# A recurrent and attention decoder trunk on one core: three early weight transfers on ScalarE's queue, fewer warm-up products, and an explicit order for the recurrent section

## The chip, the core and the metric

The kernel runs on one core of a Trainium2 chip. The metric is the device time of one execution in microseconds. The kernel before takes 560.62 us, the median of three runs (560.37 to 561.4).

## What is computed

The reference is a trunk of two layers on x of 256 positions by 1024 channels in float32. Layer 0 has a recurrent mixer (RG-LRU), layer 1 an attention mixer; each is followed by an MLP with a squared ReLU. The change lies in layer 0's mixer, which is this:

```python
h = _rmsnorm(x, norm_mix[0])
proj = h @ w_in                                   # 1024 -> 2048
y = gelu(proj[..., :D_RNN])                       # gate branch
xb = causal_depthwise_conv(proj[..., D_RNN:], conv_w, conv_b)   # width 4
r = sigmoid(einsum(xr, w_a) + b_a)                # 4 blocks of 256, xr is xb by blocks
i = sigmoid(einsum(xr, w_x) + b_x)
log_a = -RG_C * r * softplus(-lam)
u = sqrt(-expm1(2 * log_a)) * (i * xb)
hs = associative_scan(a = exp(log_a), u)          # along the positions
x = x + (hs * y) @ w_out
```

After it come the MLP of layer 0, the attention layer, its MLP and a last RMSNorm, which the change does not touch.

## The kernel before, in words

Activations lie transposed: a tile of 128 channels by 256 positions is a chunk, and x is eight chunks, `xt[:, 0]` to `xt[:, 7]`. Weights stream from memory in pieces of 128 by 1024 float32 (512 KB), in the order in which they are used, into five buffers `raw0` to `raw4`. One piece holds the eight 128 by 128 blocks of one chunk of outputs.

Products are made in three passes of a rounded format, so that float32 accuracy is kept. Every operand is split: a high part is a copy in fp32r (`split`, L426 for a cast on ScalarE or VectorE), a low part is the difference of the raw value and the high one (L423, VectorE only). There are seven pairs of buffers for split weights, called `whl` in the profile. The products of one block are high by high, high by low and low by high: `mm3`, lines L413, L414 and L415, each with 256 columns. A projection of a chunk is 8 × 3 = 24 products. In the MLP two of the three passes go together (`mm2`, L419 and L420).

The input goes through the norm's gain alone first: `hh[:, k]` is the high part of g·x (ScalarE, L681) and `hl[:, k]` the low part (VectorE, L683); the factor 1/rms of each position is applied to the results, when the sums of squares (squares on ScalarE, L687) are known.

The recurrent section consists of steps that are put into a plan by `add`, with the engine, the step's keys for reading and writing, and a due time. Then `emit` gives each engine its instructions in the order of the plan. In the kernel before, the plan comes from a list scheduler fed with a row of random seeds (`SEED`). Later sections use an explicit list of step numbers (`ORDER`): the same `emit` runs the steps just in the order listed, and a prime behind a number takes the step's second engine. Each engine runs its own instructions strictly in order, and waits where an operand is not there.

The steps of the section, in their rough order:

- the first transfers (`FIRST`), below;
- c0 to c7, the eight chunks of the convolution branch (`conv`). c0, c1 and c2 are made together, interleaved by k (the chunk of x), in steps of three products, while the inputs come in. Their weights are split by quarters of a piece, two blocks each; quarter q of piece i has the high part hi*i.q* and the low part lo*i.q*;
- g0 to g3, the gates (`gate`): 32 plain float32 products (64 records at L790), tanh and exp on ScalarE, products on VectorE;
- y0 to y7, the gate branch (`branch`), the scan on VectorE (`scan`), gelu and the product with y (`product`);
- out0 to out7, the projection back, with the residual and the norm for the MLP;
- the first three chunks of the MLP's up projection and the splits of six more pieces (`lead_in`).

The first transfers are written in `FIRST` as tags. x0+ is chunks 0 and 1 of x (256 KB), x2+, x4+ and x6+ the other pairs. A tag of two digits is a weight quarter: 00 is quarter 0 of piece 0 (128 KB); a plus adds the quarter behind it, so 10+ is quarters 0 and 1 of piece 1 (256 KB). `piece` is a whole piece, `vec` and `cst` are small vectors and constants:

```python
FIRST = "x0+ 00 01 x2+ 10+ 20+ x4+ 02+ x6+ 12+ 22+ piece vec cst piece"
```

All of these are issued by SyncE (SP) in this order; only the first eight columns of `vec`, the norm's gain, are issued by ScalarE (L655), ahead of its first step, a table load. While nothing has landed, TensorE multiplies a tile of zeros (`warm`, L675), `WARM` = 26 times.

Of the kernel before, what the change touches and what calls it, by code (L numbers as in the profile page):

```python
# [14 lines left out]
AF = mybir.ActivationFunctionType  # L15
# [6 lines left out]
D = 1024  # L22
# [56 lines left out]
TRANSFER = {"raw": (2.0, 1.4, 0.6), "cast": (1.6, 2.2, 0.4), "add": (2.4, 3.0, 0.5), "move": (1.4, 0.21, 0.3)}  # L79
PLACED = "ks0 kw0 q0 q1 q2".split()  # L80
NI, NFINE = 3, 3
SQN = 2
# [228 lines left out]
def trunk_kernel(ctx: ExitStack, tc: tile.TileContext, x_in, vec_in, const_in, w2_in, wts, out):  # L311
    nc = tc.nc
    ctx.enter_context(tc.manual_schedule())
    pe, dve, act, pool = nc.tensor, nc.vector, nc.scalar, nc.gpsimd
# [22 lines left out]
    raw_t = [rpool.tile([P, WMAX], F32, name="raw%d" % i) for i in range(NRAW)]  # L337
# [96 lines left out]
    class Section:  # L434


        def __init__(self, carried=True):
            flush()
            self.carried = carried
# [5 lines left out]
        def transfer(self, kind, q, d, fn, t, r=(), w=()):  # L445

            pre, took, post = TRANSFER[kind]
            if not self.carried:
                self.add(q, 1.5, fn, r=r, w=list(w) + ["loads"], t=t, lag=2.0)
                return  # L450
            self.add(q, d, fn, r=r, w=list(w) + ["loads"] * (kind == "raw"), t=t, lag=pre)
# [69 lines left out]
        def proj(self, name, idx, b, t, step, xs=None, xk=None):  # L521
            wh, wl, wk = self.weight(name, idx, t)
            z = self.bank((name, idx), b, zcols)
            xs, xk = xs or [(hh[:, k], hl[:, k]) for k in range(KC)], xk or hkey
            for i in range(4):
                def run(e, i=i):
                    for k in (2 * i, 2 * i + 1):
                        w = slice(k * P, (k + 1) * P)
                        mm3(z(), wh[:, w], wl[:, w], xs[k][0], xs[k][1], k == 0, k == KC - 1)
                self.add("pe", 0.67 if self.carried else 0.68, run, r=wk + list(xk[2 * i:2 * i + 2]), w=[("ps", b)], t=t + i * step)  # L530
            return z, ("ps", b)

        def table(self, func, t):
# [2 lines left out]
        def stats(self, srcs, t):  # L536

            b6 = [("ps", 6)]
            st = self.bank(("stats", t), 6, lambda x: x)
            for j, (x, k) in enumerate(srcs):  # L540
                self.add("pe", 0.44, lambda e, j=j, x=x: square_sums(st(), x, j == 0, j == len(srcs) - 1), r=[k], w=b6, t=t)
            self.add("act", 0.2 if self.carried else 0.15, lambda e: e.activation(rcol, st()[:, :2], AF.Sqrt, bias=epst, scale=1.0 / D), r=b6 + ["tab"],
                     w=["rcol"], t=t)
            self.add("dve", 0.1 if self.carried else 0.08, lambda e: e.reciprocal(rcol, rcol), w=["rcol"], t=t)
# [46 lines left out]
    rcol = spool.tile([P, 2], F32, name="rcol")  # L591
# [43 lines left out]

    with ExitStack() as ph:
        rg = ph.enter_context(tc.tile_pool(name="rg", bufs=1))
        sec = Section(False)
# [6 lines left out]
        def first_load(q, o, i, key, d):  # L645
            add(q, d, lambda e: (nc.scalar if e is act else nc.sync).dma_start(o, i), w=key + ["loads"] * (q == "sp"), t=-29.0, lag=1.9)
# [8 lines left out]
        nc.scalar.dma_start(vec[:, :8], vec_in[:, :8])  # L655
# [123 lines left out]
        def gate(b, t):  # L779
            ms = (2 * b, 2 * b + 1)  # L780
            xk = [("xb", m) for m in ms]
            for mo, m in enumerate(ms):
                for which, d, nm in ((0, r_t, "r"), (1, i_t, "i")):
                    bk = nextbank()
                    z = sec.bank(("gate", m, which), bk, zcols)

                    def run(e, z=z, which=which, mo=mo):
                        for k in range(2):
                            o = ((which * 2 + mo) * 2 + k) * P
                            e.matmul(z(), gw[b][:, o:o + P], xb[2 * b + k], start=k == 0, stop=k == 1)  # L790
                    add("pe", 0.87, run, r=[("gw", b)] + xk, w=[("ps", bk)], t=t + PJ * (2 * mo + which))
# [775 lines left out]
```

## Time and profile before

| | |
|---|---|
| median of three runs | 560.62 us |
| the profiled execution | 560.43 us |
| its span, first to last instruction | 558.6 us |
| granted TensorE clock, mean | 0.997 |
| memory read | 101.36 MB, 183 GB/s over the span with what is written |

The span runs from the first to the last instruction on the core. Engines are PE (TensorE's products), PEld (its weight loads), DVE (VectorE), ACT (ScalarE), POOL (GpSimd) and SP (SyncE); SPq and ACTq are the queues on which SyncE and ScalarE issue DMAs. Times of instructions are in microseconds from the span's start. The records of products overlap, since they are pipelined: 0.28 us is the length of one of 256 columns, and dense products start much closer together than that. The recurrent section with the lead-in ends at about 95 us, where the first product of the MLP's own loop starts.

### The profile page before, as it was taken

Reading aid. Unit: us, or ns where it says so; the run is one execution under the profiler, and the core shown is the slowest. Engines: PE = TensorE matmul, PEld = TensorE weight load, DVE = VectorE, ACT = ScalarE, POOL = GpSimd, SP = SyncE. Lnnn points to the kernel's source line nnn. Section 1 sums busy time; section 2 is a strip of 40 time slices with the busy share of each in tenths; the row PEclk is TensorE's granted clock in tenths of the full one; section 3 lists DMA queues with packets and bytes.
Section 4 is the critical chain, followed back from the end, with each engine's and each line's share of the span. In section 5 each row is a group of like instructions: output and inputs, shape, how many; then the busy total and the mean of one; then the engine's idle time right before and its main releaser. Section 6 shows DMA issues by size and latency. Waiting matters only on the chain.

```text
span 558.6 us, 10523 instructions
## 1 busy us (share of the span) xinstructions
PE 547.1 (98%) x3862; PEld 515.5 (92%) x3862; DVE 454.8 (81%) x943; ACT 387.3 (69%) x793; POOL 51.0 (9%) x63
## 2 busy tenths in 40 slices
PE   8999999999999999999999998999999999999994
PEld 8999999999999999999999997999999999999994
DVE  6999999999996675676999999999999996565532
ACT  7699775877775553555799999977788776453420
POOL 1210000000000221221000101000000000132320
PEclk9999999999999999999999999999999999999998
DMA  8935466766566466556650767424777656466402
GB/s 290 407 131 189 151 223 194 261 200 211 193 196 221 151 207 216 180 192 225 242 182 16 211 160 238 102 42 153 241 241 231 216 196 227 153 190 220 156 1 75
DMA packets 32611, 105.19 MB, mean 188 GB/s; under 512 B 3984, under 2 KB 6944, under 8 KB 32560
## 3 DMA queue, kind: packets, MB, share of 16 engines
q1 hardware_dynamic: 30784, 99.70, 53.0%
q0 software_dynamic: 1200, 4.29, 3.3%
q8 instruction: 30, 0.49, 0.3%
q10 hardware_dynamic: 576, 0.53, 0.3%
q14 instruction: 21, 0.17, 0.1%
HBM read 101.36 MB, written 1.05 MB: 183 GB/s over the span
## 4 chain that ended last, share of the span: by engine, by line
PE 90%; ACT 5%; DVE 2%; DMA 1%; issue 1%; SPq 0%; DVEq 0%; ACTq 0%
PE bank L419 35%; PE bank L420 18%; PE bank L414 9%; PE bank L413 9%; PE bank L415 9%; PE bank L790 2%; ACT pt L1278 2%; PE bank L1308 1%; DMA xt<-in_dram 1%; ACT pth L1311 1%; PE bank L1335 1%; PE bank L1268 1%; PE bank L1140 1%; PE bank L1138 1%; PE bank L1139 1%
## 5 line engine op out<-in xcount | busy, mean ns | idle before, releaser
L369 DVE TENSOR_TENSOR whl<-raw,whl 128x1024 fp32r<-128x1024 f32 x117 | 146.5, 1272 | 5.5 <-ACT whl L360 3.1
L419 PE MATMUL bank<-hhl,whl 128*128 128x512 f32 x456 | 149.5, 382 | 0.0
L419 PE MATMUL bank<-uhl,whl 128*128 128x512 f32 x448 | 146.8, 382 | 0.0
L360 ACT CAST whl<-raw 128x1024 fp32r<-128x1024 f32 (+1 forms) x118 | 120.5, 1046 | 7.8 <-ACT whl L360 5.7
L420 PE MATMUL bank<-hhl,whl 128*128 128x256 f32 x456 | 124.3, 273 | 0.0
L420 PE MATMUL bank<-uhl,whl 128*128 128x256 f32 x448 | 122.1, 273 | 0.0
L419 PEld LDWEIGHTS bank<-hhl,whl 128*128 128x128 f32 x456 | 86.2, 189 | 11.9
L419 PEld LDWEIGHTS bank<-uhl,whl 128*128 128x128 f32 x448 | 84.7, 189 | 11.8
L413 PE MATMUL bank<-hhl,whl 128*128 128x256 f32 x312 | 87.9, 282 | 0.3 <-ACT hhl L681 0.3
L420 PEld LDWEIGHTS bank<-hhl,whl 128*128 128x128 f32 x456 | 87.6, 192 | 0.0
L414 PE MATMUL bank<-hhl,whl 128*128 128x256 f32 x312 | 86.1, 276 | 0.1
L420 PEld LDWEIGHTS bank<-uhl,whl 128*128 128x128 f32 x448 | 86.0, 192 | 0.0
L415 PE MATMUL bank<-hhl,whl 128*128 128x256 f32 x312 | 85.8, 275 | 0.0
L633 DVE TENSOR_TENSOR xt<-xt,bank 128x256 f32<-128x256 f32 x40 | 16.1, 417 | 72.2 <-ACT part L921 58.8
L423 DVE TENSOR_TENSOR whl<-raw,whl 128x1024 fp32r<-128x1024 f32 (+3 forms) x69 | 72.8, 1072 | 0.8 <-ACT whl L426 0.7
L426 ACT CAST whl<-raw 128x1024 fp32r<-128x1024 f32 (+2 forms) x61 | 57.0, 954 | 6.2 <-DMA raw<-in_dram 3.6
L414 PEld LDWEIGHTS bank<-hhl,whl 128*128 128x128 f32 x312 | 59.7, 191 | 0.9 <-DVE hhl L683 0.5
L413 PEld LDWEIGHTS bank<-hhl,whl 128*128 128x128 f32 x312 | 59.7, 191 | 0.7 <-ACT hhl L681 0.4
L415 PEld LDWEIGHTS bank<-hhl,whl 128*128 128x128 f32 x312 | 59.7, 191 | 0.0
L921 ACT COPY part<-bank 128x256 f32<-128x256 f32 x14 | 5.2, 372 | 61.8 <-PE bank L420 61.8
L893 ACT ACTIVATE u<-t 128x256 f32<-128x256 f32 x64 | 26.7, 418 | 12.3 <-DVE t L891 7.1
L886 ACT COPY b<-bank 128x256 f32<-128x256 f32 x57 | 20.9, 366 | 18.4 <-PE bank L420 18.3
(219 smaller groups left out, 1000.2 us busy)
## 6 DMA issues: line engine op xcount, KB each, us to landing
raw<-in_dram SPq DMA_DIRECT2D x171, 512.0 KB, 4.3
whl<-in_dram POOLq DMA_DIRECT2D x8, 512.0 KB, 5.4
gw<-in_dram SPq DMA_DIRECT2D x4, 512.0 KB, 8.9
raw<-in_dram SPq DMA_DIRECT2D x5, 256.0 KB, 5.4
xt<-in_dram SPq DMA_DIRECT2D x4, 256.0 KB, 4.9
zwol<-in_dram SPq DMA_DIRECT2D x2, 512.0 KB, 5.9
raw<-in_dram SPq DMA_DIRECT2D x2, 456.0 KB, 3.9
kh<-th SPq DMA_DIRECT2D x8, 64.0 KB, 5.1
```

The source lines that it names most:

```text
L360: (act.copy if eng is None else eng.tensor_copy)(hi_t[i % NSPL][:, :n], raw_t[i % NRAW][:, :n])
L369: (eng or dve).tensor_tensor(lo[:, :n], raw_t[i % NRAW][:, :n], hi[:, :n].bitcast(F32), op=OP.subtract)
L413: pe.matmul(ps, wh, xh, start=start, stop=False)
L414: pe.matmul(ps, wh, xl, start=False, stop=False)
L415: pe.matmul(ps, wl, xh, start=False, stop=stop)
L419: pe.matmul(z.rearrange("p (i b a) -> p i b a", i=2, a=2), wh, xd, start=start, stop=False)
L420: pe.matmul(pairs(z[:, :S]), wl, xd[:, 0], start=False, stop=stop)
L423: return lambda e: e.tensor_tensor(o, a, h.bitcast(F32), op=OP.subtract)
L426: return lambda e: (e.copy if e is act else e.tensor_copy)(o, a)
L633: dve.tensor_tensor(two(xt[:, m]), two(xt[:, m]), nat(z), op=OP.add)
L886: act.copy(two(b), nat(z[:, S:]))
L893: act.activation(u, t, AF.Square)
```

## The change

Four things are changed together.

1. Three of the first transfers, 00, 01 and 10+, are issued by ScalarE instead of SyncE, right behind its transfer of `vec`, and so ahead of its table load. The other transfers stay on SyncE in the order that they had.
2. `WARM` is 22 instead of 26.
3. The section's order comes from an explicit list of step numbers, `RG_STEPS`, and no longer from the scheduler with its seeds. The steps themselves are the same. A transfer is now two steps, the issue and the time on the DMA engines, and the second gives no instruction.
4. Some of the scheduler's costs are changed. With an explicit list they give no instruction and set no order.

The list of all 510 entries is cut here to its first two lines:

```diff
-SEED = (45, 94848, 51544, 88889, 49550, 67068, 32457, 33019)
+RG_STEPS = """
+1 5 4 8 2 111 112 6 9 0 11 13 15 17 53 19 32 54 21 29 33 59' 23 30 55' 60 25 35 113 56 38 27 114 36 61' 126 39 57' 127
+62 44 115 58 65' 116 63 41 128 66 129 71' 64 139 47 42 140 67' 72 141 73' 45 142 174 69' 117 48 43 118 50 68 119 74 40
...
+"""
-WARM = 26
+WARM = 22
...
         def first_w(i, q, n=2):
             w = wts[offs[i]:offs[i + 1]].rearrange("(h p n) -> h p n", h=2, p=P)[q // 2][:, q % 2 * 256:(q % 2 + n) * 256]
-            first_load("sp", raw_t[i][:, q * 256:(q + n) * 256], w, [("raw0", i, q + j) for j in range(n)], (0.47, 0.68)[n - 1])
-        sec.plan.busy["pool"] = 0.9
+            key = [("raw0", i, q + j) for j in range(n)]
+            if q + i < 2:
+                nc.scalar.dma_start(raw_t[i][:, q * 256:(q + n) * 256], w)
+                add("sp", 0.0, lambda e: None, w=key, t=-31, lag=3.2 + 0.4 * q + 1.2 * i)
+                return
+            first_load(raw_t[i][:, q * 256:(q + n) * 256], w, key, 0.34 * n)
+        sec.plan.busy.update(pool=0.9, sp=0.74, act=2.1, pe=5.2, dma=2.3)
...
-        sec.emit(SEED)
+        sec.emit(RG_STEPS)
```

With the steps' names in place of their numbers, the list begins like this on each engine:

- SyncE: x0+, x2+, 20+, x4+, 02+, x6+, 12+, 22+, piece, vec, cst, piece
- ScalarE: table load, hh1, hh0, hi0.1, hi1.0, hh2, hh3, hi1.1, hi2.0, hh5, hi0.2, hh4, hi0.3, hh6, hi1.2
- VectorE: hi0.0, lo0.0, hl1, hl0, lo0.1, lo1.0, hl2, hl3, lo1.1, lo2.0, hi2.1, lo0.2, lo2.1, hl4, lo0.3
- TensorE: c0 k0, c0 k1, c1 k0, c1 k1, c0 k2, c0 k3, c1 k2, c1 k3, c2 k0, c2 k1, c2 k2, c2 k3, c0 k4, c0 k5

Of the wide high parts of the pieces from c3 to the last of the lead-in, the list gives 26 to ScalarE and four to VectorE: those of y6 and of the up pieces 3, 5 and 7.

More of the change, by code (lines that the diff above doesn't have):

```diff
@@ L38 @@
 W1T, THS, THD, TPV, THT, NEARLY = 8.0, 10.5, 6.4, 44.0, 5.6, 6
-SEED = (45, 94848, 51544, 88889, 49550, 67068, 32457, 33019)
+RG_STEPS = """
+1 5 4 8 2 111 112 6 9 0 11 13 15 17 53 19 32 54 21 29 33 59' 23 30 55' 60 25 35 113 56 38 27 114 36 61' 126 39 57' 127
+62 44 115 58 65' 116 63 41 128 66 129 71' 64 139 47 42 140 67' 72 141 73' 45 142 174 69' 117 48 43 118 50 68 119 74 40
[6 rows of a table added]
+296 256 337' 241 288 229 258 272 346 289 338 268 243 259 266 245 273 347 260 297 267 270 269 262 274 303 246 271 390 329
[3 rows of a table added]
+445 352 369 490 383 394 368 498 387 432 384 417 385' 454 418 386 419 468 407 455 395 446 480 408 506 433 409 520 481 456
+411 492 420 434 524 457 447 421 469 410 422 396 448 470 399 449 482 412 508 493 458 500 459 423 528 483 397 460 435 501
+471 424 461 484 398 532 485 436 509 472 494 425 536 473 495 450 486 437 462 502 487 438 474 503 451 463 475 526 496 488
+464 510 476 477 504 522' 511 489 530' 497 514 512 523 515 505 516 540 534 517 538' 513 531 518 544 519 527 539 550 545
+552 542 543 546 535 554 556 547 548 549
+"""
 ORDER = """
@@ L76 @@
 RPEN = 0.51
-WARM = 26
+WARM = 22
 BY_DMA, DLEAD, NPEN = "o01 o03 o11 o13", 12.0, 0.3
-TRANSFER = {"raw": (2.0, 1.4, 0.6), "cast": (1.6, 2.2, 0.4), "add": (2.4, 3.0, 0.5), "move": (1.4, 0.21, 0.3)}
+TRANSFER = {"first": (1.5, 0.67, 0.7), "raw": (2.0, 1.3, 0.6), "cast": (1.6, 2.2, 0.4), "add": (2.4, 3.0, 0.5), "move": (1.4, 0.21, 0.3)}
 PLACED = "ks0 kw0 q0 q1 q2".split()
@@ L443, in __init__, with transfer @@
             self.zs = {}
-        def transfer(self, kind, q, d, fn, t, r=(), w=()):
+        def transfer(self, kind, q, d, fn, t, r=(), w=(), size=None):
             pre, took, post = TRANSFER[kind]
[L448 to L451, printed above, removed]
+            self.add(q, d, fn, r=r, w=list(w) + ["loads"] * (kind in ("raw", "first")), t=t, lag=pre)
             self.plan.carried[len(self.plan.tasks)] = len(self.plan.tasks) - 1
-            self.add("dma", took, lambda e: None, r=r, w=w, t=t, lag=post)
+            self.add("dma", took if size is None else size, lambda e: None, r=r, w=w, t=t, lag=post)
         def load(self, i, t):
@@ L529, in run @@
                         mm3(z(), wh[:, w], wl[:, w], xs[k][0], xs[k][1], k == 0, k == KC - 1)
-                self.add("pe", 0.67 if self.carried else 0.68, run, r=wk + list(xk[2 * i:2 * i + 2]), w=[("ps", b)], t=t + i * step)
+                self.add("pe", 0.67, run, r=wk + list(xk[2 * i:2 * i + 2]), w=[("ps", b)], t=t + i * step)
             return z, ("ps", b)
@@ L541, in stats @@
                 self.add("pe", 0.44, lambda e, j=j, x=x: square_sums(st(), x, j == 0, j == len(srcs) - 1), r=[k], w=b6, t=t)
-            self.add("act", 0.2 if self.carried else 0.15, lambda e: e.activation(rcol, st()[:, :2], AF.Sqrt, bias=epst, scale=1.0 / D), r=b6 + ["tab"],
+            self.add("act", 0.2, lambda e: e.activation(rcol, st()[:, :2], AF.Sqrt, bias=epst, scale=1.0 / D), r=b6 + ["tab"],
                      w=["rcol"], t=t)
-            self.add("dve", 0.1 if self.carried else 0.08, lambda e: e.reciprocal(rcol, rcol), w=["rcol"], t=t)
+            self.add("dve", 0.1, lambda e: e.reciprocal(rcol, rcol), w=["rcol"], t=t)
             self.add("pe", 0.22, lambda e: spread(st()), r=["rcol", "cst"], w=b6, t=t)
@@ L643, in trunk_kernel, with first_load @@
         table(AF.Sqrt, -30)
-        def first_load(q, o, i, key, d):
-            add(q, d, lambda e: (nc.scalar if e is act else nc.sync).dma_start(o, i), w=key + ["loads"] * (q == "sp"), t=-29.0, lag=1.9)
+        def first_load(o, i, key, took):
+            sec.transfer("first", "sp", 0.46, lambda e: e.dma_start(o, i), -29.0, w=key, size=took)
         def first_x(k, n=2):
-            first_load("sp", xt[:, k:k + n], x_in[k // 2], [("xt", k + i) for i in range(n)], (0.47, 0.68)[n - 1])
+            first_load(xt[:, k:k + n], x_in[k // 2], [("xt", k + i) for i in range(n)], 0.67 + 0.5 * (k == 2))
         def first_w(i, q, n=2):
             w = wts[offs[i]:offs[i + 1]].rearrange("(h p n) -> h p n", h=2, p=P)[q // 2][:, q % 2 * 256:(q % 2 + n) * 256]
-            first_load("sp", raw_t[i][:, q * 256:(q + n) * 256], w, [("raw0", i, q + j) for j in range(n)], (0.47, 0.68)[n - 1])
-        sec.plan.busy["pool"] = 0.9
+            key = [("raw0", i, q + j) for j in range(n)]
[5 more added lines that the diff above has]
+        sec.plan.busy.update(pool=0.9, sp=0.74, act=2.1, pe=5.2, dma=2.3)
         nc.scalar.dma_start(vec[:, :8], vec_in[:, :8])
-        add("sp", 0.0, lambda e: None, w=["vec0"], t=-31, lag=2.2)
+        add("sp", 0.0, lambda e: None, w=["vec0"], t=-31, lag=3.1)
         sec.seen.update(dma=NFINE, split=NFINE, lo=NFINE)
@@ L662, in trunk_kernel @@
             elif x == "cst":
-                first_load("sp", cst, const_in, ["cst"], 1.0)
+                first_load(cst, const_in, ["cst"], 0.78)
             elif x == "vec":
-                first_load("sp", vec[:, 8:], vec_in[:, 8:], ["vec"], 0.47)
+                first_load(vec[:, 8:], vec_in[:, 8:], ["vec"], 0.24)
             elif x[0] == "x":
@@ L790, in run @@
                             e.matmul(z(), gw[b][:, o:o + P], xb[2 * b + k], start=k == 0, stop=k == 1)
-                    add("pe", 0.87, run, r=[("gw", b)] + xk, w=[("ps", bk)], t=t + PJ * (2 * mo + which))
+                    add("pe", 0.865, run, r=[("gw", b)] + xk, w=[("ps", bk)], t=t + PJ * (2 * mo + which))
                     j = which * 8 + m
```

5 lines of the change are left out of this document (2 added, 3 removed), and 9 rows, old and new, of the table RG_STEPS.

## The prediction

> **What bounds the kernel now.** I read the page first: the span and the busy engines.
>
> ```profile
> span 558.6 us, 10523 instructions
> PE 547.1 (98%) x3862; PEld 515.5 (92%) x3862; DVE 454.8 (81%) x943; ACT 387.3 (69%) x793; POOL 51.0 (9%) x63
> ```
>
> TensorE (PE) is busy for 98% of the span. The profiled execution took 560.43 us, 1.8 us more than its span, and the median of the runs is 560.62 us, so a microsecond saved in the profile is a microsecond of the median. Next the windows view, by stage, for where PE is not busy. Its columns are the stretch, its length, busy time of PE, weight loads, VectorE (DVE), ScalarE (ACT) and GpSimd, the granted clock, the DMA engines' busy share and GB/s.
>
> ```profile
> core 0: us, PE busy (x) PEld busy (x) DVE busy (x) ACT busy (x) POOL busy (x), PEclk, DMA share, GB/s
> 0.00:1.50 1.50, 0.36 (x1) 0.37 (x2) 0.06 (x1) 0.33 (x1) 0.65 (x9) 1.00 0.00 0
> 1.50:3.50 2.00, 2.00 (x11) 2.00 (x11) 0.00 (x0) 1.16 (x2) 0.00 (x0) 1.00 0.77 205
> 3.50:5.00 1.50, 1.50 (x9) 1.50 (x9) 0.87 (x3) 1.12 (x3) 0.00 (x0) 1.00 0.72 175
> 5.00:12.00 7.00, 6.60 (x52) 6.04 (x51) 5.90 (x18) 5.54 (x17) 0.00 (x0) 1.00 1.00 365
> 12.00:30.00 18.00, 18.00 (x155) 17.70 (x154) 17.42 (x46) 13.48 (x25) 4.83 (x6) 1.00 1.00 390
> 30.00:56.00 26.00, 26.00 (x183) 24.55 (x182) 25.56 (x42) 25.59 (x47) 2.07 (x5) 1.00 0.44 153
> 56.00:95.00 39.00, 39.00 (x352) 39.00 (x351) 38.03 (x65) 28.32 (x45) 0.00 (x0) 1.00 0.53 178
> ```
>
> From 12 us to the end of the section at 95 us PE has no idle time, and DVE idles only 0.58 + 0.44 + 0.97 = 1.99 us. What a new order can win is therefore in the first 12 us, and what it can lose is anywhere after them. The DMA engines are full from 5 us on, but move only 205 and 175 GB/s between 1.5 and 5 us. The waits of the first 9 us (us in total, times, longest) say what PE lacks there:
>
> ```profile
> DVE whl L426 <- DMA raw<-in_dram: 3.2, 1, 3.2
> ACT hhl L681 <- DMA xt<-in_dram: 1.4, 1, 1.4
> DVE hhl L683 <- ACT hhl L681: 1.1, 1, 1.1
> PEld bank L414 <- DVE hhl L683: 0.5, 2, 0.3
> PEld bank L413 <- ACT hhl L681: 0.4, 1, 0.4
> ```
>
> PE waits for DVE and ACT, which make the high and low parts of x (hh, hl), and those wait for x in the DMA. The timeline of the same time shows the chain (start, length, engine, line, operation; SPq and ACTq are DMA issues):
>
> ```profile
> 0.73 0.41 ACTq L655 DMA_DIRECT2D vec<-in_dram  x1
> 0.74 0.39 SPq L646 DMA_DIRECT2D xt<-in_dram  x1
> 1.14 5.26 PE L675 MATMUL bank<-warm 128*128 128x256 f32 x26 [1.14 <-POOL xp L740]
> 1.18 1.28 ACT L534 ACT_TABLE_LOAD   x1 [1.18 <-PEq L1556]
> 1.18 0.89 SPq L646 DMA_DIRECT2D raw<-in_dram  x2
> 2.12 0.43 SPq L646 DMA_DIRECT2D xt<-in_dram  x1
> 2.59 0.91 SPq L646 DMA_DIRECT2D raw<-in_dram  x2
> 3.54 0.43 SPq L646 DMA_DIRECT2D xt<-in_dram  x1
> 3.88 0.91 ACT L681 ACTIVATE hhl<-xt,vec 128x256 fp32r<-128x256 f32 x2 [1.21 <-DMA vec<-in_dram]
> 4.09 0.29 DVE L426 CAST whl<-raw 128x256 fp32r<-128x256 f32 x1 [3.22 <-DMA raw<-in_dram]
> 4.42 0.48 DVE L683 SCALAR_TENSOR_TENSOR hhl<-xt,vec,hhl 128x256 fp32r<-128x256 f32 x1
> 5.05 0.48 DVE L683 SCALAR_TENSOR_TENSOR hhl<-xt,vec,hhl 128x256 fp32r<-128x256 f32 x1
> 5.44 0.76 DVE L423 TENSOR_TENSOR whl<-raw,whl 128x256 fp32r<-128x256 f32 x2
> 6.12 0.19 PEld L413 LDWEIGHTS bank<-hhl,whl 128*128 128x128 f32 x1
> 6.76 0.91 ACT L681 ACTIVATE hhl<-xt,vec 128x256 fp32r<-128x256 f32 x2 [1.35 <-DMA xt<-in_dram]
> ```
>
> In the order of the queue the transfers are x0+, 00, 01, x2+, 10+, 20+, x4+. The first product starts at 6.12; the second pair of x chunks (x2+, issued fourth) is there at 6.76. Counting the products that read the split weights:
>
> ```profile
> 6.12:8.43 2.31, 1.80 (x10) 1.00 0.98 337
> 8.43:12.83 4.40, 4.40 (x40) 1.00 1.04 395
> ```
>
> Dense, 40 products take 4.40 us, 0.11 each. In the 2.31 us before that only 10 were done, for 1.10 us of work: 1.2 us are lost. The first three pieces are 72 products, so they end at about 8.43 + 62 × 0.11 = 15.25 us.
>
> **The change, part by part.** *The three weight transfers.* 00, 01 and 10+ leave SP's queue for ACT's. On SP each issue takes 0.47 us (0.74, 1.18 and two, 2.12), so x2+ is issued at 1.18 instead of 2.12, and x4+ at about 2.1 instead of 3.54. On ACT three issues stand behind that of vec and take 3 × 0.43 = 1.3 us. Behind them is queued the table load, and behind that hh1 and hh0: the load ends near 0.73 + 4 × 0.45 + 1.28 + 0.1 = 3.9 us. ACT was idle for 1.21 us until 3.88, so this costs nothing; were x0+ there sooner than 3.6 us, it would cost the difference.
>
> *The first product.* The list has DVE make hi0.0 (high part of piece 0, quarter 0), lo0.0, hl1, hl0, in that order, and takes the casts of the other early quarters off it. If 00 lands at 4.1 to 4.6 us (4.09 before; it now shares the engines with x2+), the product follows after 0.33 + 0.38 + 0.40 + 0.40 + 0.1 = 1.6 us, at 5.7 to 6.2. I take 5.9: 0.2 us sooner.
>
> *The four warm-ups.* 26 of them take from 1.14 to 6.12, 0.19 each. The last four are worth between 4 × 0.11 = 0.44 and 0.76 us, so 22 end between 5.36 and 5.68, before the inputs are there. They take nothing off the sum by themselves; kept, they would hold the first product at 6.12.
>
> *What is late next: 10+.* The list puts two steps of piece 0 first (k0, k1: six products, 0.66 us), then k0 of piece 1, on PE; hi1.0 ahead of hh2 and hh3 on ACT; lo1.0 ahead of hl2 and hl3 on DVE. All three engines run in order, so x2+ is of no use until 10+ has landed. Call that time T. Then
>
> ```profile
> L426 ACT CAST whl<-raw 128x256 fp32r<-128x256 f32 x8 | 3.0, 395 | 0.1
> L423 DVE TENSOR_TENSOR whl<-raw,whl 128x256 fp32r<-128x256 f32 x12 | 4.5, 421 | 0.0
> ```
>
> the high part takes 0.40 and the low part 0.42 us, and the seventh product starts at T + 0.85. The remaining 66 products end at T + 0.85 + 66 × 0.11 = T + 8.1, if everything else is in time. Before it was 15.25. So the gain is 7.15 − T, and no more than the start allows: 15.25 − (5.9 + 72 × 0.11) = 1.4 us.
>
> For T, the landings (KB each, us from issue to landing; x0+, x2+, 10+, x4+):
>
> ```profile
> xt<-in_dram SPq DMA_DIRECT2D x1, 256.0 KB, 2.9
> xt<-in_dram SPq DMA_DIRECT2D x1, 256.0 KB, 4.6
> raw<-in_dram SPq DMA_DIRECT2D x1, 256.0 KB, 4.8
> xt<-in_dram SPq DMA_DIRECT2D x1, 256.0 KB, 5.2
> ```
>
> x0+ lands at 0.74 + 2.9 = 3.64. x2+ lands at 6.7 and x4+ at 8.74, with 10+ and 20+ between: three transfers of 256 KB in 2.0 us, 0.67 each, which is the full rate. x2+ itself comes 3.1 us behind x0+, though only 512 KB (1.35 us) lie between: there the engines had nothing to do, as the share of 0.72 says. 10+ is issued on ACT at about 2.05. It cannot be there before 2.05 + 2.9 = 4.95. Behind 00, 01 and x2+ it lands at 3.64 + 768 KB = 5.65; with 20+ ahead of it too at 6.3; with x4+ as well at 7.0. I take T = 5.9, between the second and the third and nearer to the second, since x2+ is issued 0.5 us before 20+ and two queues are served by turns. The gain is 7.15 − 5.9 = 1.25 us.
>
> *The others.* 20+, x4+, 02+ and what follows are issued 1.4 us sooner and land about 1 us sooner, because the rate is full from then on and only the empty time can be won. The list asks for 02+ fourth from there; if it is late by 0.5 us the gain is 0.75 us.
>
> *The order after 12 us.* It is the same set of steps. In the list ACT makes 26 of the 30 wide high parts and DVE four; before, ACT made all 30 up to 95 us. DVE has no such row, and its nearest one is the half-width cast:
>
> ```profile
> L426 ACT CAST whl<-raw 128x1024 fp32r<-128x1024 f32 x30 | 30.5, 1046 | 5.0 <-DMA raw<-in_dram 3.6 <-PE bank L414 1.4
> L426 DVE CAST xbh<-y 128x512 fp32r<-128x512 f32 x1 | 0.4, 429 | 0.0
> ```
>
> so four cost DVE at most 4 × 0.86 = 3.4 us, more than the 1.99 us that it idles after 12 us. Three of the four stand at the very end of the section, behind the last hl, where DVE no longer gates the last products; their cover is the start of the MLP, and if that is gone they cost up to 3 × 0.86 − 1.99 = 0.6 us. From below, a better order could win nothing, as PE has no wait there. I take 0, and for the range 0.4 us of loss. A gain in the section passes to the end: the stages behind it are chained by buffers and not by the clock.
>
> Sum: 560.43 − 1.25 = 559.2 for a profiled execution, 559.4 for the median.
>
> **The rivals.** All but one turn on T.
> (1) *Cover holds*, T below 5.7: the start limits, gain 1.4 to 1.7 us (with a first product at 5.7), 559.0. For it: x0+ lands 2.9 us after its issue, and 00 does too (1.18 to the cast at 4.09). Against it: 768 KB stand before 10+.
> (2) *The queues only take turns.* If SP's x2+, 20+ and x4+ are each served before ACT's next one, T = 7.0 and the gain is 0.15 us: 560.5. For it: the share of 1.00 from 5 us on, which no second queue raises. Against it: the 0.72 before. The Trainium skill, "DMA: Bandwidth & Descriptors", section "Issuing engines are not separate DMA queues", states that issuing from several engines only saves the issuing time, since all share the same 16 engines. By that rule this is the whole case, and the time would be the 560.5 of this rival; the trace agrees as to the full rate after 5 us, and not for the time before.
> (3) *Slower: 10+ starves.* If SP's queue is served first throughout, up to x6+, then five transfers of 256 KB, 00 with 01, and 10+ itself follow x0+, and T = 3.64 + 7 × 0.67 = 8.3, and by the same formula the kernel loses 1.2 us: 561.8. It turns slower than before from T = 7.15 on. Against it: 10+ landed at 2.59 + 4.8 = 7.39 as the fifth of one queue, and now it is the fourth of its own.
> (4) *It does not do what it says:* the start is sooner, but the gain is given back between 30 and 56 us, where ACT is busy 25.59 of 26.00 us and DVE 25.56. Against it: the list takes work off ACT there.
>
> **How the numbers follow.** The measurement of this kernel tells 0.2% (1.1 us) from no change. Forecast, T between 5.7 and 6.4, gain 0.75 to 1.4: 0.50, of which 0.33 is over 1.1 us. Rival 1: 0.21, all faster. Rival 2: 0.14 and rival 4: 0.07, both no change. Rival 3 and any worse order: 0.08, slower. Faster 0.33 + 0.21 = 0.54; the same 0.17 + 0.21 = 0.38; slower 0.08. The range reaches from rival 1 at its most (1.7 us) and the 0.3 us by which the fastest run before lay under the median, 558.6, to rival 2 with 0.2 us of the order's loss, 560.7; out of it lie rival 3 and a tenth at the edges. Faster cases and no change hold most of it; the likeliest case's own range is 559.0 to 559.9.
>
> **What would show it.** The ACT queue with four issues before the table load, which ends near 3.9 us; x2+ issued at 1.18; hh2 started before 6.76, at about T + 0.35; a first product at 5.7 to 6.2; the seventh at T + 0.85; the 72nd near 14.0. The wait for 10+ should be ACT's (hi1.0) and PE's longest after the first product. The forecast is wrong if T is over 6.5, if PE has idle time after 15 us, or if PE stands after the sixth product for anything else than 10+.

## The result and the profile after

The changed kernel takes **564.5 us**, the median of six runs (562.88 to 565.91); the kernel before, run beside it, 560.55 us (559.85 to 561.4). The ratio is **1.0071, with a 95% interval of 1.005 to 1.0092**: it is slower, by some 4 us, where 1.2 us of gain were forecast. The spread belongs to the kernel: three of the six runs had a mean granted clock of 0.992 or 0.993 and took 564.9 to 565.9 us, three had 0.995 or 0.996 and took 562.9 to 564.1; the experiments show what goes with it. The profiled execution is one of the first kind, 564.93 us.

The line numbers have moved: products L431 to L433 (before L413 to L415), split casts L444 (L426), low parts L441 (L423), hh L700, hl L702. The page's head, then the stages in the windows view (length; busy PE, PEld, DVE, ACT, POOL; granted clock; DMA share; GB/s):

```profile
span 563.2 us, 10517 instructions
PE 549.4 (98%) x3858; PEld 516.7 (92%) x3858; DVE 455.2 (81%) x946; ACT 382.2 (68%) x790; POOL 49.4 (9%) x63
```

```profile
5.00:12.00 7.00, 5.39 (x28) 4.84 (x28) 5.05 (x15) 4.20 (x12) 0.00 (x0) 0.81 0.95 352
12.00:30.00 18.00, 17.99 (x158) 17.80 (x158) 15.56 (x34) 13.20 (x26) 0.74 (x4) 0.98 0.99 362
30.00:56.00 26.00, 25.11 (x163) 22.89 (x163) 24.15 (x50) 22.79 (x44) 4.57 (x8) 1.00 0.34 122
56.00:95.00 39.00, 39.00 (x351) 38.95 (x350) 37.58 (x64) 27.19 (x44) 0.00 (x0) 1.00 0.54 189
```

PE has lost time in two places above all: between 5 and 12 us it starts 28 products instead of 52 (those of zeros among them), at a mean clock of 0.81, and between 30 and 56 us, where it had been full, it is idle for 0.89 us. The timeline of the beginning, without PE:

```profile
0.74 0.41 ACTq L674 DMA_DIRECT2D vec<-in_dram  x1
0.74 0.86 SPq L660 DMA_DIRECT2D xt<-in_dram  x2
1.18 1.41 ACTq L669 DMA_DIRECT2D raw<-in_dram  x3
2.63 1.28 ACT L548 ACT_TABLE_LOAD   x1 [2.63 <-issue]
3.75 0.33 SPq L660 DMA_DIRECT2D raw<-in_dram  x1
4.76 0.29 DVE L444 CAST whl<-raw 128x256 fp32r<-128x256 f32 x1 [3.89 <-DMA raw<-in_dram]
7.36 0.33 SPq L364 DMA_DIRECT2D raw<-in_dram  x1
7.36 0.41 ACT L444 CAST whl<-raw 128x256 fp32r<-128x256 f32 x1 [2.44 <-DMA raw<-in_dram]
8.20 0.33 SPq L660 DMA_DIRECT2D vec<-in_dram  x1
8.21 0.41 ACT L444 CAST whl<-raw 128x256 fp32r<-128x256 f32 x1 [0.44 <-DMA raw<-in_dram]
```

The casts show the landings of ScalarE's three transfers: 00 at 4.76, 01 at 7.36 and 10+ at 8.2 us. PE, in the same view:

```profile
5.96 0.27 PE L431 MATMUL bank<-hhl,whl 128*128 128x256 f32 x1
6.91 0.28 PE L433 MATMUL bank<-hhl,whl 128*128 128x256 f32 x1
8.66 0.38 PE L431 MATMUL bank<-hhl,whl 128*128 128x256 f32 x1 [1.48 <-ACT whl L444]
9.36 0.43 PE L431 MATMUL bank<-hhl,whl 128*128 128x256 f32 x1
9.58 0.42 PE L432 MATMUL bank<-hhl,whl 128*128 128x256 f32 x1
```

The first product starts right behind the last product of zeros (5.79), the second waits for its low part until 6.36. The sixth starts at 6.91, the seventh at 8.66, as soon as the cast of 10+ allows. Then they come 0.22 us apart instead of 0.11. The windows view of PE alone says why (length, PE busy, granted clock, DMA share, GB/s; the last three in full, with all engines):

```profile
5.90:9.31 3.41, 1.80 (x11) 1.00 1.01 380
```

```profile
9.00:10.00 1.00, 1.00 (x6) 0.88 (x5) 1.00 (x4) 1.00 (x5) 0.00 (x0) 0.66 1.02 377
10.00:11.00 1.00, 1.00 (x6) 1.00 (x6) 1.00 (x4) 1.00 (x4) 0.00 (x0) 0.50 0.98 381
13.00:14.00 1.00, 1.00 (x12) 1.00 (x11) 1.00 (x5) 1.00 (x4) 0.00 (x0) 1.00 0.80 285
```

The clock's record in the trace begins at 5.90 us and changes at 9.31 and 12.72: full and half for 3.41 us each, then full again. Ahead of its first entry the view prints 1.00, but there the products of zeros start 0.21 us apart, as the products do in the half-clock stretch; behind it they start 0.12 apart (in e1 below, whose record begins at 4.01 us). So the beginning runs at half speed, up to a moment that differs from run to run, 4.01 to 7.30 us in these traces. And what comes later, from the waits (us in total, times, longest; the second line belongs to the sum of squares near 23 us, the others to the gates near 40 us):

```profile
ACT t L818 <- POOL sp L747: 2.4, 1, 2.4
DVE rcol L558 <- ACT rcol L556: 2.3, 1, 2.3
PE bank L431 <- ACT r L812: 0.9, 1, 0.9
```

To see where the time goes in every kernel, the products behind the warm-ups are numbered in the order of their records. The table gives the start of the n-th, for the kernel before in us from the span's start, for the others as its lag behind that (minus: earlier). Number 73 follows the three first pieces, 109 to 157 the sum of squares, 193 to 321 the gates, 737 lies twelve products into the MLP's own loop. While the gates run the orders differ, so only columns outside them compare. In all rows but e2 the first product stands right behind the last product of zeros, so column 1 tells mainly when full speed set in, which is chance.

| kernel | 1 | 7 | 25 | 73 | 109 | 157 | 321 | 705 | 737 |
|---|---|---|---|---|---|---|---|---|---|
| before, start | 6.23 | 7.32 | 10.10 | 15.63 | 19.65 | 25.00 | 49.98 | 92.86 | 97.06 |
| **the change** | -0.27 | +1.35 | +2.47 | +2.37 | +2.37 | +2.60 | +3.96 | +4.09 | +4.55 |
| e1_list_sp | -1.10 | -0.36 | -0.80 | +0.17 | +0.56 | +1.05 | +2.43 | +2.57 | +3.31 |
| e2_old_order_act | -0.66 | +1.85 | +1.94 | +1.77 | +1.77 | +1.77 | +1.77 | +1.77 | +1.77 |
| e3_fill (zeros not counted) | -0.26 | +1.08 | +0.65 | +0.55 | +0.57 | +1.31 | +2.67 | +2.82 | +2.82 |
| e4_old_order_sp | -0.26 | -0.54 | -0.54 | -0.17 | -0.17 | -0.17 | -0.17 | -0.17 | -0.17 |
| f1_head_sp | -0.87 | -0.04 | -0.47 | -0.57 | +1.09 | +1.09 | +1.09 | +1.09 | +1.09 |
| f2_tail_sp | -0.56 | -0.22 | -0.48 | -0.01 | -0.01 | +0.40 | +1.72 | +1.87 | +2.19 |
| f3_third_on_sp | -0.37 | +0.11 | -0.30 | -0.43 | -0.41 | +0.34 | +1.71 | +1.86 | +2.42 |
| f4_small_early | -0.24 | +1.36 | +0.92 | +0.82 | +0.84 | +1.45 | +1.56 | +1.56 | +1.73 |
| g1_mended | -0.23 | -0.07 | -0.84 | -1.00 | -0.98 | -0.98 | -0.98 | -0.98 | -0.98 |
| g2_old_order_two | -0.85 | +0.32 | -0.02 | -0.07 | -0.07 | -0.07 | -0.07 | -0.07 | -0.07 |
| g3_quarters | -0.35 | -0.77 | -1.07 | -0.41 | -0.15 | +2.25 | +4.08 | +4.08 | +4.30 |
| h1_mended_three | -0.23 | +1.27 | +0.83 | +0.73 | +0.75 | +0.75 | +0.84 | +0.84 | +0.84 |

The change's own row is the account: 1.35 us at the seventh product, 2.37 by the 73rd, then 0.23 more at the sum of squares, 1.36 in the gates, 0.13 and 0.46 towards the end. What follows is the same for all: from the first product of the MLP's loop to the end the change takes 463.6 us, before 463.5. One run of g2_old_order_two, slow at 812 us and a clock of 0.654, is left out of its ratio.

### The profile page after: what moved, and what is told of

Its sections match the earlier page's. It is cut to its first block, busy times and chain, and to the rows that moved or that the text cites. A ratio compares the mean times of both kernels' runs of the same rounds, so it can differ in the third digit from the quotient of the medians.

```text
span 563.2 us, 10517 instructions
## 1 busy us (share of the span) xinstructions
PE 549.4 (98%) x3858; PEld 516.7 (92%) x3858; DVE 455.2 (81%) x946; ACT 382.2 (68%) x790; POOL 49.4 (9%) x63
## 3 DMA queue, kind: packets, MB, share of 16 engines
q10 hardware_dynamic: 1008, 1.05, 0.5%
HBM read 101.36 MB, written 1.05 MB: 182 GB/s over the span
## 4 chain that ended last, share of the span: by engine, by line
PE 81%; ACT 6%; DVE 3%; DMA 1%; issue 1%; DVEq 0%; ACTq 0%
PE bank L437 35%; PE bank L438 17%; PE bank L431 7%; PE bank L432 7%; PE bank L433 7%; ACT pt L1297 2%; PE bank L1327 1%; PE bank L809 1%; DMA raw<-in_dram 1%; ACT whl L444 1%; ACT pth L1330 1%; PE bank L1354 1%; PE bank L1287 1%; PE bank L1159 1%; PE bank L1157 1%
## 5 line engine op out<-in xcount | busy, mean ns | idle before, releaser
L431 PE MATMUL bank<-hhl,whl 128*128 128x256 f32 x312 | 89.0, 285 | 2.4 <-ACT whl L444 1.5
L433 PE MATMUL bank<-hhl,whl 128*128 128x256 f32 x312 | 86.7, 278 | 0.0
L441 DVE TENSOR_TENSOR whl<-raw,whl 128x1024 fp32r<-128x1024 f32 (+3 forms) x69 | 73.1, 1072 | 3.3 <-ACT whl L444 3.2
L431 PEld LDWEIGHTS bank<-hhl,whl 128*128 128x128 f32 x312 | 60.5, 194 | 3.3 <-ACT whl L444 1.7
L444 ACT CAST whl<-raw 128x1024 fp32r<-128x1024 f32 (+2 forms) x58 | 53.7, 937 | 11.4 <-DMA raw<-in_dram 8.7
L433 PEld LDWEIGHTS bank<-hhl,whl 128*128 128x128 f32 x312 | 60.4, 194 | 0.2 <-DVE whl L441 0.2
```

The lines of the kernel that those rows point to most:

```text
L431: pe.matmul(ps, wh, xh, start=start, stop=False)
L433: pe.matmul(ps, wl, xh, start=False, stop=stop)
L441: return lambda e: e.tensor_tensor(o, a, h.bitcast(F32), op=OP.subtract)
L444: return lambda e: (e.copy if e is act else e.tensor_copy)(o, a)
```

## The experiments

Theory A: the second queue makes 10+ late, the list lets everything wait for it, and the idle TensorE then loses its clock. Theory B: the list loses by itself, later in the section. A2 and B2 are the same, sharpened by the first four runs. All kernels have 22 warm-up products; "old order" is the order of before, written as a list, which gives the same instructions. Where transfers are put on SyncE again, this is the edit, with `ON_ACT` as each experiment says:

```diff
+ON_ACT = set()                  # or {(0, 0), (0, 1)}, or with (1, 0) as in the change
...
+            if q + i < 2 and (i, q) not in ON_ACT:
+                add("sp", 0.5, lambda e: e.dma_start(raw_t[i][:, q * 256:(q + n) * 256], w), w=key, t=-29.0)
+                return
             if q + i < 2:
```

**e1_list_sp: the new list, all transfers on SyncE.** Edit: `ON_ACT = set()`, and

```diff
-1 5 4 8 2 111 112 6 9 0 11
+1 2 4 5 111 112 6 8 9 0 11
```

> The new order with all first transfers back on SyncE, in the old order of transfers, 22 warm-ups. Theory A (the second queue makes 10+ late, and the list lets everything wait for 10+): 10+ lands near 7.4 us as it did before the change instead of 8.2, the seventh product starts near 8.3 instead of 8.66, and if the granted clock then stays at 1.0 the time is 560.9 to 561.5 us, with the clock halved again 562.5 to 563. Theory B (the list loses by itself, behind the start, between 30 and 56 us): 564 us, as the change.

Measured: 562.7 us, 1.0047 (1.0032 to 1.0062). There is no second queue, and it is still slower. The beginning is early and then late, level at the 73rd product; 0.9 us go at the sum of squares, 1.4 in the gates, 0.9 at the end. So theory A alone does not do, and a good half of the loss goes with the list.

**e2_old_order_act: the old order, three transfers on ScalarE.** Edit: the old order for the list, `ON_ACT` with all three.

> The old order of all steps with 00, 01 and 10+ on ScalarE's queue, 22 warm-ups. Theory A: 01 lands late too (7.4 us), so the third step starts near 8.2 instead of 7.3, PE is idle for 1.2 us or more, and the time is 561 to 563 us, slower than before without any new order. Theory B: x2+ is there at 4.6, so the start is sooner, 560 us or less.

Measured: 562.46 us, 1.0036 (1.0021 to 1.005). All the loss comes ahead of the 25th product, and none behind it. Five of its seven runs had a clock of 0.991 or 0.992 and took 562.4 to 563.7 us; two had 0.996 and 0.994 and took 560.6 and 560.9, against 560.16 for the kernel before beside them. So without the half clock the queue costs little here, although PE waits for a late weight in this order too:

```profile
PE bank L434 <- DVE whl L442: 1.9, 1, 1.9
```

**e3_fill: the change, with twelve products of zeros behind the sixth product.** Edit: `F12` in the list behind step 114, and

```diff
+                if x[0] == "F":
+                    self.fill(int(x[1:]))
+                    continue
...
+        sec.plan.fill = lambda n: [pe.matmul(wz, warm[:, :P], warm, start=True, stop=True) for _ in range(n)]
```

> The changed kernel with twelve products of zeros put behind the sixth product, where TensorE is idle for 1.5 us, and nothing else. Theory A with the clock as its second term: the arrival of 10+ and the start of the seventh product stay (8.66 us), the granted clock stays at 1.0 from 9.3 to 12.7 us, and the time falls by 1.7 us to 562.8. Theory B: the clock is a side effect whose loss is hidden by the later waits, 564.5 us.

Measured: 563.21 us, 1.0053 (1.0034 to 1.0071). 10+ is as late as before (seventh product +1.08), but the clock stays full, and the lag at the 73rd product is 0.55 instead of 2.37 us. The half clock is a cost of its own. In the medians this is 1.0 us by the ratios, with intervals that overlap, since only three of the six runs of the change have the lower clock and none of the four here.

**e4_old_order_sp: before, with 22 warm-up products.** Edit: the old order, `ON_ACT = set()`.

> The kernel before with 22 warm-ups instead of 26 and nothing else. Both theories: the first product starts up to 0.2 us sooner, the second pair of chunks of x still lands at 6.7, so 560.3 to 560.7 us, no difference.

Measured: 560.14 us, 0.9999 (0.999 to 1.0008). Four warm-ups fewer cost and bring nothing.

**f1_head_sp: the new list up to the last product of c2, the old order behind it; all on SyncE.** Edit: the two lists joined there.

> All transfers on SyncE; the new list up to the last product of c2, then the remaining steps in the order that they had before. Theory B2 (the new list loses in its later part, at the sums behind c2 and in the gate stage, and its beginning neither wins nor loses): the 72nd product comes 0.2 us later than before, as in the whole list on SyncE (15.80 us against 15.63), the MLP loop starts at 95.3 us against 95.09, and the time is 560.4 us, 560.0 to 560.8. Theory C (the new beginning itself upsets what follows: HI and LO of c3 and c4 and the sums come late on ACT and DVE because its casts stand ahead of them): the wait at the sum of squares, 0.9 us in the whole list, stays, and the time is 561.2 us or more.

Measured: 562.07 us, 1.0029 (1.0019 to 1.004). The expectation of B2 failed. The beginning is 0.57 us early at the 73rd product, and then PE stands at the sum of squares (L640). Its line in the waits:

```profile
PE bank L640 <- DVE x L722: 1.4, 1, 1.4
```

The list makes three of the squares behind HI c4, and its own sum stands later than the old one. Here the two parts did not fit each other: the joined list has a wait that neither whole has.

**f2_tail_sp: the old order up to the last product of c0 to c2, the new list behind it; all on SyncE.** Edit: joined the other way round.

> All transfers on SyncE; the order of before up to the last product of c0 to c2, then the remaining steps in the order of the new list. Theory B2: the gate stage loses the 1.4 us that it loses in the whole list (products 193 to 321: +1.05 to +2.43 us), the sums behind c2 and at the end up to 1.5 us more; the MLP loop starts between 96.5 and 98.2 us and the time is 561.6 to 563.2 us, 562.3 taken. Theory C: 560.2 us, as before with 22 warm-up products.

Measured: 562.83 us, 1.0043 (1.0029 to 1.0058). From a beginning that is level (-0.01) the list loses 0.41 us at the sums, 1.32 in the gates and 0.47 at the end. That is theory B by itself.

**f3_third_on_sp: the change, with only 10+ back on SyncE, behind x2+.** Edit: `ON_ACT = {(0, 0), (0, 1)}`, and

```diff
-1 5 4 8 2 111 112 6 9 0 11
+1 5 4 2 111 112 6 8 9 0 11
```

> The changed kernel, with 10+ issued by SyncE right behind x2+ and only 00 and 01 by ScalarE. Theory A2 (10+ is late because it is third on the ScalarE queue, takes turns with 20+ and x4+ of the SyncE queue, and the idle TensorE then gets half the clock for 3.4 us): 10+ lands at 6.0 to 6.6 us instead of 8.2, the seventh product starts at 6.4 to 7.0 us instead of 8.66, TensorE's clock is not halved, the 72nd product starts 1.5 to 2.4 us earlier than in the changed kernel, and the time is 562.3 us, 561.8 to 563.0. Rival Q (any weight transfer on a second queue makes the beginning late by the same amount, because the queues share the 16 rings): the seventh product at 8 us or later, 564 us or more.

Measured: 563.33 us, 1.0047 (1.0032 to 1.0062). The seventh product is at 7.42 and the 73rd at 15.20, 2.8 us earlier than in the change and earlier than before. The time falls by 1.2 us only, outside the range expected, because the list now loses 2.85 us behind it, 0.77 of them at the sums: there ScalarE makes HI c7 first, as in the change. That the loss is larger than the change's 2.2 us because the beginning is earlier was not tried by itself.

**f4_small_early: the change, with nine small VectorE operations moved up.** Edit, the part of VectorE's order that changes:

```diff
-97 151 98 182 99 100 160 101 171 161 184 102 162 185 103 172 104 186 105 173
+97 151 98 99 182 100 101 102 160 103 104 105 171 161 184 162 185 172 186 173
```

> The changed kernel, with nine 128x8 operations on VectorE (97 to 105) ahead of the causal-convolution steps of m = 3, 4 and 5 and not spread behind them; transfers as in the changed kernel. Theory B2 (in the gate stage the ACT t step waits 2.4 us for POOL, whose four operations wait for the last of these nine; the tanh behind it on ACT then frees a bank 0.9 us late): POOL's last four start about 2 us earlier, the waits of 2.4 us on ACT and 0.9 us on TensorE go, the lag behind before stays near +2.6 us at product 321 instead of 3.96, the MLP loop starts at 98.2 us instead of 99.56, and the time is 563.2 us, 562.6 to 563.9. Rival G (the gate stage is short of ACT or VectorE time in this order, so that another bank is freed late): the lag at product 321 stays 3.5 us or more, and the time is 564.2 us or more.

Measured: 562.41 us, 1.0032 (1.0021 to 1.0044). The four GpSimd operations that wait for the ninth, in the change and then here:

```profile
35.82 1.54 POOL L744 TENSOR_SCALAR sp<-sp 128x8 f32<-128x8 f32 x1 [5.03 <-DVE sp L743]
37.44 0.20 POOL L745 TENSOR_TENSOR sp<-sp,sp 128x8 f32<-128x8 f32 x1
37.73 0.23 POOL L746 TENSOR_SCALAR sp<-sp 128x8 f32<-128x8 f32 x1
38.04 1.11 POOL L747 TENSOR_SCALAR sp<-sp 128x8 f32<-128x8 f32 x1
```

```profile
32.29 0.40 POOL L748 TENSOR_SCALAR sp<-sp 128x8 f32<-128x8 f32 x1 [2.64 <-DVE sp L747]
32.78 0.28 POOL L749 TENSOR_TENSOR sp<-sp,sp 128x8 f32<-128x8 f32 x1
33.15 0.34 POOL L750 TENSOR_SCALAR sp<-sp 128x8 f32<-128x8 f32 x1
33.57 0.31 POOL L751 TENSOR_SCALAR sp<-sp 128x8 f32<-128x8 f32 x1
```

They end at 33.88 instead of 39.15. The waits of 2.4 us on ACT and 0.9 us on PE are gone, and the gates cost 0.11 us (from 1.45 to 1.56) instead of 1.36. The profiled run also kept its full clock, with the same program ahead of 25 us. The time is a little below the range expected. Of the six runs three had a clock of 0.996 or 0.997 and took 561.8 to 562.5 us, three had 0.991 or 0.992 and took 562.4 to 563.2: the half clock goes with less here, 0.6 us between the medians, and why was not tried.

**g1_mended: f3 and f4 together, and two more places mended.** On ScalarE HI c7 stands behind `rs` and no longer ahead of `rcol`; on VectorE LO c7 stands behind the xp steps, and HI up3 and HI up5 behind the last sum of squares. Edit besides f3's and f4's, in terms of the list:

```diff
 ScalarE
-202 83 87 86
+83 87 86 202
 VectorE
-84 203 190 134 121 147
+84 190 134 121 147 203
-522' 489 530' 514
+489 514 522' 530'
```

> The kernel with 10+ back on SyncE, and three places of the new list mended: the nine small VectorE operations early (as in f4), HI c7 on ACT behind rs instead of ahead of rcol (LO c7 behind the xp steps), HI up3 and HI up5 on VectorE behind the final sum of squares. Theory B2 with A2 (the loss of the change is the late third transfer with its halved clock and these three places, and nothing else): the lag behind before stays where the beginning leaves it, -0.4 us at the 73rd product, within 0.3 us to the MLP loop, which starts at 94.5 to 95.2 us; the time is 560.0 us, 559.5 to 560.6. Rival G (behind 17 us ScalarE and VectorE have no slack in this order, so that mending one place only makes the next one late): the lag at product 737 stays over 1 us, and the time is 561.3 us or more.

Measured: 560.06 us, ratio 0.9993 (0.9984 to 1.0003). The only wait of PE that the view names up to 100 us is the one of the warm-ups, and the lag of -0.98 at the 109th product is still -0.98 at the 737th. So the late 10+ and these three places of the list hold the whole loss of the change; the two places mended here were not tried one by one. It beats the change by 4.4 us. The kernel before it does not measurably beat: the lead of 0.98 us is that of the profiled run, which took 559.43 us and is the fastest of ten, and the medians differ by 0.2 us.

**g2_old_order_two: the old order, 00 and 01 on ScalarE, 10+ on SyncE.** Edit: the old order, `ON_ACT = {(0, 0), (0, 1)}`.

> The order of before with 00 and 01 on ScalarE and 10+ on SyncE, 22 warm-up products. Theory A2 (the second queue only hurts by the third transfer, which is as large as the first two together): no idle stretch of TensorE over 1.2 us between 6 and 10 us, no halved clock, the lag at the 73rd product -0.3 to +0.5 us, and the time is 560.3 us, 559.9 to 560.9. Rival Q (any weight transfer on the ScalarE queue makes a later one late): lag +1.5 us or more as with three transfers, and 561.5 us or more.

Measured: 560.83 us, 1.0015 (1.0001 to 1.003). The lag is -0.02 at the 25th product and -0.07 from the 73rd on. At full clock a second queue as such does no harm, and no good; it is the third transfer. The half clock can strike here too: two of nine runs had 0.992 and took 562.7 and 563.2 us, seven had 0.994 to 0.997 and took 560.3 to 560.9.

**g3_quarters: another order of the beginning, for more gain.** Edit, besides a list for it:

```diff
-FIRST = "x0+ 00 01 x2+ 10+ 20+ x4+ 02+ x6+ 12+ 22+ piece vec cst piece"
+FIRST = "x0+ 00 10 20 x2+ 01 11 21 x4+ 02+ 12+ 22+ x6+ piece vec cst piece"
```

> All transfers on SyncE, in the order x0+ 00 10 20 x2+ 01 11 21 x4+ 02+ 12+ 22+ x6+: the first quarters of all three channel blocks come ahead of x2+, the products run k by k over the three blocks, the sum of squares stands behind c4, the rest is the mended list. Theory B2: each group of 18 products then needs two parts of the input and three quarters of weights, about 2.1 us of ScalarE and of VectorE for 2.0 us of products, TensorE starts at 5.0 to 5.6 us and does not wait long again, the 73rd product starts at 13.6 to 14.6 us (15.63 before), 1 us or more of this is kept, and the time is 559.0 us, 558.3 to 559.9. Rival G (no slack on ScalarE and VectorE behind 14 us): the 73rd product is as early, but the lag is back at -0.3 us or above by the gate stage, and the time is 560.0 us or more.

Measured: 564.65 us, 1.0077 (1.0058 to 1.0096). 1.5 us ahead at the 13th product, level by the 97th, and then a wait of 2.2 us at the sum of squares and 1.2 us in the gates. Neither forecast described it: the 73rd product came at 15.22 us and not by 14.6, so that most of the lead was gone ahead of the squares. In time it is on rival G's side, and why this list waits was not tried further.

**h1_mended_three: g1's list with all three transfers on ScalarE.** Edit: g1 without f3's part.

> The changed kernel with its three transfers on ScalarE, and the three places of its list mended as in the kernel that has 10+ on SyncE and the same list. Theory A2 with B2 (two separate losses that add): 10+ lands at about 8.2 us again and the seventh product starts at 8.4 to 8.8 us; the lag at the 73rd product is +0.7 to +1.0 us where the granted clock stays at 1.0 and +2.3 to +2.5 where it is halved, and it stays within 0.4 us of that to the MLP loop; the time is 562.0 us, 561.3 to 562.8. Rival (the mended list has slack behind 17 us, so that a late beginning is caught up or the products behind hide it): 560.8 us or less. Rival G (the three places were mended only for a beginning that is early): a new wait over 0.5 us behind 17 us, 563 us or more.

Measured: 561.36 us, 1.0021 (1.0009 to 1.0033). The seventh product is late again (+1.27), and the profiled run, at full clock, keeps +0.73 to +0.84 to the end. Of ten runs three had a clock of 0.992 and took 562.6 to 563.0 us, seven had 0.994 to 0.997 and took 560.8 to 561.6: 1.75 us between their means, about half of 3.41.

## Why the prediction was wrong

- **What bounds the kernel.** It held: before the change PE was full from 12 us on, only the first 12 us could be won, and anything behind them could be lost. In g1's profiled run the whole lead, 0.98 us, was won ahead of the 73rd product.
- **ScalarE's three issues.** Right: 1.41 us for the three (1.3 said), the table load ended at 3.91 (3.9). **x2+** was issued at 1.18, as said.
- **The first product.** 5.96 against 5.9, but by luck: its operands were ready at 5.05, and what held it was the last product of zeros. The forecast had the 22 of them end by 5.68, from a mean of 0.19 us; at half speed they start 0.21 us apart. The chain that it worked out ends with the second product, at 6.36, since 00 landed at 4.76 and not at 4.1 to 4.6. **The warm-ups.** Nothing in the total, as said (e4).
- **"I take T = 5.9, between the second and the third."** This is the step that failed first. 10+ landed at 8.2 us. Its price of 8.1 us from T to the 72nd product was about right: in h1 and f4, at full clock, the 73rd product started at 16.36 and 16.45, which is T + 8.2. The reason for T is in the DMA view of the change for 3.1 to 8.2 us (packets, MB, share of 16 engines; q1 is SyncE's queue, q10 ScalarE's):

```profile
q1 hardware_dynamic: 682, 1.24, 66.4%
q10 hardware_dynamic: 441, 0.52, 29.2%
```

While ScalarE's half megabyte moved, SyncE's queue moved 1.24 MB, mostly x2+, 20+, x4+ and 02+. The five transfers from x0+ to 10+ in the old order are 1.05 MB; here it was 0.28 (moved before 3.1 us) + 1.24 + 0.52 = 2.0 MB, at about 0.35 MB a microsecond. The forecast let the queues take turns but counted x4+ and 02+ out. Put on SyncE again, 10+ lands at 1.66 + 4.2 = 5.9 us (in g1, one transfer, us from issue to landing):

```profile
raw<-in_dram SPq DMA_DIRECT2D x1, 256.0 KB, 4.2
```

That is the T of the forecast, and g1's 73rd product at 14.62 is a gain of 1.0 us in that run, against the 1.25 worked out for it; in the medians it is between 0.9 us of gain and 0.2 us of loss. So what a given T costs was right, and T was wrong. The rule of the Trainium skill that the prediction cited, "DMA: Bandwidth & Descriptors", section "Issuing engines are not separate DMA queues", fits the runs: two transfers on the second queue won nothing (g2, -0.07 us). That the third lands later there, at 8.2 us for 5.9, is what the traces add.
- **Rival 2** had the mechanism, turns, and gave it T = 7.0 by counting x0+, x2+, 20+ and x4+ on SyncE's queue, 1.05 MB; the trace has 0.28 + 1.24 = 1.52 MB, with 02+ and more behind it, and T = 8.2.
- **Rival 3** named the time, T = 8.3 and 561.8 us, at 0.08. Its reason, that SyncE is served first throughout, is not what the trace shows: both queues moved at the same time, though SyncE's 1.24 MB to ScalarE's 0.52. h1, where this is the only loss, takes 561.36. So the sign that the prediction set, wrong if T is over 6.5, came true, and so did the other, PE idle after 15 us.
- **The clock** was in no term and no rival. It costs 1.6 us in the profiled run: 2.37 us of lag at the 73rd product, against 0.73 and 0.82 in h1 and f4, which begin in the same way at full clock. That is near the 1.75 us by which h1's two kinds of runs differ. With the change's own list part of it is hidden later: at the 157th product the lag is 2.60, against 1.45 in f4.
- **"I take 0, and for the range 0.4 us of loss"**, for the order after 12 us: this failed as well. f2 measures it alone: 2.2 us of lag, 562.83 us. Three places carry it, and each was in the list to be read: HI c7 ahead of `rcol` on ScalarE, the nine small operations behind the convolution steps on VectorE with GpSimd and the ACT `t` step behind them, and HI up3 and HI up5 ahead of the last sum. The second is shown by itself (f4), the other two only together (g1, h1). The first place in the change, on ScalarE:

```profile
21.85 1.05 ACT L444 CAST whl<-raw 128x1024 fp32r<-128x1024 f32 x1 [1.87 <-DMA raw<-in_dram]
22.80 0.26 ACT L556 ACTIVATE rcol<-bank,epst 128x2 f32<-128x2 f32 x1
```

The third, on VectorE, and the sum that waits for it:

```profile
95.53 0.69 DVE L444 CAST whl<-raw 128x1024 fp32r<-128x1024 f32 x1
96.13 0.42 DVE L571 TENSOR_TENSOR sq<-xt 128x256 f32<-128x256 f32 x1
96.46 0.69 DVE L444 CAST whl<-raw 128x1024 fp32r<-128x1024 f32 x1
97.06 0.41 DVE L582 TENSOR_TENSOR acc<-acc,sq 128x256 f32<-128x256 f32 x1
97.53 0.60 PE L639 MATMUL bank<-ones,acc 128*128 128x1 f32 x4 [0.19 <-DVE acc L582]
```

Of the wide casts on VectorE the forecast said that three stand behind the last hl, where VectorE gates nothing. They do stand there, and their length was within its bound (0.68 us each, at most 0.86 said). But two stand ahead of the sum that everything waits for, and 0.46 us were lost there.
- **Rival 4** had the place, 30 to 56 us, at 0.07, but priced it at no change. The argument against it, that the list takes work off ScalarE, was no argument: ScalarE did less (22.79 us busy for 25.59) because it waited; in g1, with the same list but for the three places and without the wait, it was busy for 25.32.

The sum as it was: 2.4 us in the beginning instead of -1.25, and 2.2 us in the list instead of 0, makes 4.55 us of lag in the profiled run; without the half clock about 3, and the median of 4 us lies between. The prediction's first step that failed is thus T, 8.2 us for 5.9, and its second the order after 12 us, 2.2 us for 0; the half clock came on top.

## What to carry to other kernels

A transfer moved to a second, emptier queue is not moved ahead: count every byte that both queues hold until it lands, and if a strict order makes everything wait for that one transfer, leave it where it is. An order written out in full is checked on each engine for the small step that a long chain hangs on, and for wide work ahead of a reduction; a busy share of 98% does not show these. Losses at different places added up only roughly: behind the 73rd product the new list lost 2.2 us in the change and in f2, 2.85 in f3 and 3.1 in e1. So look at the lag of the n-th product, which shows where a loss arises, and not at totals alone.

## What the runs showed of the hardware

**A window that is only partly idle can halve the clock of the next.** The Trainium skill, "TensorE: Matmul & The Clock Gate", section "Part 1: The HAM clock gate", has free-running windows of 3413 ns and a half clock after a window of idling. The length agrees (3.41 us, beginning at another time in each run, which fits that only some runs are struck); in the condition the traces differ, if idling means no products at all. The change's window from 5.90 to 9.31 had PE busy for 1.80 us and was followed by half speed. So was one of e2 (first row, then a microsecond behind it):

```profile
4.16:7.57 3.41, 1.87 (x12) 1.00 0.99 363
9.00:10.00 1.00, 1.00 (x6) 1.00 (x6) 1.00 (x4) 1.00 (x4) 0.00 (x0) 0.50 1.06 358
```

One of f4 was not (first row, then a microsecond behind it), nor was one of g3 (last row), although PE is busy there for less than in e2 and idle for 1.8 us on end:

```profile
6.54:9.95 3.41, 2.09 (x14) 1.00 1.03 390
10.00:11.00 1.00, 1.00 (x11) 1.00 (x10) 1.00 (x4) 1.00 (x4) 0.00 (x0) 1.00 1.04 405
19.38:22.79 3.41, 1.62 (x15) 1.00 1.03 414
```

So the busy time as the view counts it gives no bound. By their number of products these four would order (11 and 12 struck, 14 and 15 not), but a window at e2's end with 17 (550.28 to 553.70, PE busy for 1.99 us) was followed by half speed. What the clock goes by stays open; that the idle stretch of 1.5 us in the change matters is shown by e3, where products of zeros in it kept the clock.

**Eight transfers in flight over both queues, in this program.** In the change eight transfers are issued by 2.6 us, four by each engine, and SyncE issues the ninth only at 3.75, when the first, vec, has landed (0.74 + 3.0). Its issues at 7.36 and 8.20 stand at the landings of 01 and 10+. So a late transfer on ScalarE seems to hold back SyncE's as well. Whether the program or the hardware sets this was not tried.

**A small GpSimd operation ended with the VectorE operation beside it.** The 128x8 operation that took 0.40 us in f4 took 1.54 in the change, and the one that took 0.31 took 1.11. In the change VectorE made a wide low part (128x1024, 1.2 us) at those times, and the GpSimd operation ended 0.09 us behind it both times; in f4 it made convolution steps of 128x256. The late chain was 1.7 us longer for it (3.33 us for 1.59). It was seen in these rows only, and not tried by itself.
